# Mixer input projection by Strassen's scheme over 1024 tokens, attention beside the output projection of the chunk ahead

## Chip, cores and metric

The kernel runs on one core of a Trainium2 chip. The metric is the device time of one execution in microseconds; the time before is the median of three executions. One further execution was recorded by the profiler, and all rows of the profile come from it.

## The reference

One decoder layer for 2048 tokens of width 1024, all in float32. `w_in` has 4352 columns: queries (512), keys (128), values (128), three convolution inputs (512 each) and two gates (1024 each).

```python
def reference(x, mix_norm, w_in, b_in, sinks, conv_w, w_attn_branch, w_conv_branch, w_out,
              ffn_norm, w_up, ffn_conv_w, w_down, final_norm):
    h = x
    ...
        xn = rms_norm(h, mix_norm[l])
        proj = jnp.einsum("bsd,dp->bsp", xn, w_in[l]) + b_in[l]
        q, k, v, cb, cc, cx, ga, gc = jnp.split(proj, splits, axis=-1)
        attn = sliding_window_attention(q, k, v, sinks[l])
        conv = cb * causal_depthwise_conv(cc * cx, conv_w[l])
        merged = (jax.nn.sigmoid(ga) * jnp.einsum("bsc,cd->bsd", attn, w_attn_branch[l])
                  + jax.nn.sigmoid(gc) * jnp.einsum("bsc,cd->bsd", conv, w_conv_branch[l]))
        h = h + jnp.einsum("bsd,de->bse", merged, w_out[l])
        hn = rms_norm(h, ffn_norm[l])
        up = causal_depthwise_conv(jnp.einsum("bsd,df->bsf", hn, w_up[l]), ffn_conv_w[l])
        gate, val = jnp.split(up, 2, axis=-1)
        h = h + jnp.einsum("bsf,fd->bsd", jax.nn.silu(gate) * val, w_down[l])
    return rms_norm(h, final_norm)
```

Attention has 8 query heads on 2 key heads of width 64. Each block of 128 queries sees itself and the block before, under a band mask of 128 keys, and each head has a sink logit in its softmax. The convolutions are causal with three taps.

## The kernel before

Everything lies transposed: 128 channels on the partitions, tokens along the row. The sequence is worked in four chunks of 512 tokens; `k` counts the 8 slices of 128 channels of the width 1024. A float32 value is split into a high part, rounded to the type the matmul takes, and the rest (`split`, lines 221 to 223: a cast on ScalarE, a subtraction on VectorE). A product is then three matmuls, high by high, high by low and low by high (`mm3`, lines 197 to 199). Weights come as tiles of 128 columns (512 KB raw, 1 MB split); `order` lists them in the order of their use, `fetch` (line 121) loads and splits one, and `prefetch` runs two tiles ahead in the mixer and three in the feed-forward part. All transfers are issued on SyncE's queue (SP), one after the other. A scheduler places the instructions of each engine by its own model, so their order is near that of the code but not the same.

For each chunk `mixer` (line 466) projects keys, values and queries (`mixer_inputs`, line 320), then runs four blocks of attention: `scores` (line 373: scores and softmax), `weights_to_keys` (line 405: transposes of the weights and their split), `attend` (line 418: the product with the values). Between them stand the projections of the convolution inputs (`conv_tiles`, line 432). Eight branch steps follow, each with two gate projections (`gate`, line 460), the product of the convolution and that of the attention with the branch weights. `fillers` (line 506) slips in, beside the branch steps, the sums of squares of the next chunk and, in chunks 2 and 3, the operands of the up-projection of the first 1024 tokens (two slices in each). `out_proj` (line 530) adds x, stores h and normalizes it, and prepares the next chunk's input.

The up-projection already runs by the Strassen-Winograd scheme (`up`, line 608): over 1024 tokens a pair of weight tiles takes 7 products of 12 matmuls where plain products take 8. `up_operands` (line 564) forms the seven operands of the tokens by sums, splits them and stores them in DRAM; `load_up` (line 602) loads them as tiles of 2 MB, the first four ahead of the last output projection. The sums of weights are formed beside the products (`fetch_sums`). `down` (line 700) is plain; during its first half the operands of the second 1024 tokens are formed.

## Time and profile before

| | |
|---|---|
| median of three executions | 2550.72 us (2547.49 to 2550.80) |
| profiled execution, its own time | 2549.53 us |
| its span (first to last instruction) | 2547.8 us |
| mean granted clock of TensorE | 0.996 |
| transfers | 394.23 MB, 155 GB/s over the span |

The span leaves out some 2 us at the ends of an execution. Busy shares are means over stages with different limits, so a stage is read from its own stretch. In the page, PE is the matmul side of TensorE and PEld its weight loads, DVE is VectorE, ACT ScalarE, POOL GpSimd, and a row of a group ends with the idle time of the engine before it and what ended that.

### The profile page before, as it was taken

How to read it: one execution, taken by the hardware profiler on the slowest of the kernel's cores; microseconds unless marked ns; L12 is line 12 of the kernel's file. 1: busy time of each engine (PE TensorE's matmuls, PEld its weight loads, DVE VectorE, ACT ScalarE, POOL GpSimd, SP SyncE). 2: the span in 40 equal slices, each digit the busy share in tenths (PEclk: the TensorE clock that was granted, in tenths of full speed). 3: DMA queues.
4: the chain of work that ended last, by engine and by line, in shares of the span. 5: the costliest groups of instructions: out<-in, count | busy, mean ns of one | idle time of the engine just before them, and what ended most of it. 6: DMA issues, size and time to landing. Idle time of an engine off the chain costs nothing.

```text
span 2547.8 us, 29898 instructions
## 1 busy us (share of the span) xinstructions
PE 2525.5 (99%) x11404; PEld 2094.8 (82%) x11404; DVE 1711.5 (67%) x2093; ACT 1086.7 (43%) x1723; POOL 22.1 (1%) x73
## 2 busy tenths in 40 slices
PE   9999999999999999999999999999999999999998
PEld 7888888888888888887888888888888888888886
DVE  7954677446865568634798888755478888875335
ACT  6543455334653345432555555422135555551001
POOL 0000000000000000000000000000000000000000
PEclk9999999999999999999999999999999999999998
DMA  5243533335256442747443233888463333356421
GB/s 151 75 153 96 163 116 118 124 104 177 76 190 206 142 142 72 269 137 278 151 150 115 100 116 116 296 311 297 179 230 124 111 121 100 110 194 255 176 83 66
DMA packets 133631, 394.23 MB, mean 155 GB/s; under 512 B 15600, under 2 KB 16752, under 8 KB 128624
## 3 DMA queue, kind: packets, MB, share of 16 engines
q1 hardware_dynamic: 133488, 392.33, 45.5%
q8 instruction: 89, 1.46, 0.2%
q14 instruction: 54, 0.44, 0.1%
HBM read 291.61 MB, written 100.66 MB: 154 GB/s over the span
## 4 chain that ended last, share of the span: by engine, by line
PE 98%; issue 1%; DVE 0%; DMA 0%; ACT 0%; SPq 0%; POOLq 0%; POOL 0%; DVEq 0%; ACTq 0%
PE upx L620 6%; PE upx L622 6%; PE upx L621 6%; PE dn L197 6%; PE dn L199 6%; PE dn L198 6%; PE g L197 5%; PE g L199 5%; PE g L198 5%; PE upz L621 3%; PE upz L622 3%; PE upz L620 3%; PE wo L199 2%; PE wo L197 2%; PE wo L198 2%; PE upy L622 2%
## 5 line engine op out<-in xcount | busy, mean ns | idle before, releaser
L223 DVE TENSOR_TENSOR wh<-wr,wh 128x1024 fp32r<-128x1024 f32 (+1 forms) x250 | 298.6, 1197 | 228.3 <-ACT wh L222 226.3
L222 ACT CAST wh<-wr 128x1024 fp32r<-128x1024 f32 (+1 forms) x250 | 256.1, 1026 | 424.3 <-PE dn L199 214.4
L622 PE MATMUL upx<-upx,wh 128*128 128x512 f32 x704 | 275.8, 392 | 1.9 <-DVE wh L223 1.9
L620 PE MATMUL upx<-upx,wh 128*128 128x512 f32 x704 | 276.3, 393 | 0.0
L621 PE MATMUL upx<-upx,wh 128*128 128x512 f32 x704 | 275.6, 392 | 0.0
L197 PE MATMUL dn<-act,wh 128*128 128x512 f32 x704 | 274.2, 390 | 0.0
L199 PE MATMUL dn<-act,wh 128*128 128x512 f32 x704 | 274.0, 389 | 0.0
L198 PE MATMUL dn<-act,wh 128*128 128x512 f32 x704 | 273.9, 389 | 0.0
L713 DVE TENSOR_TENSOR hr<-dn,hr 128x512 f32<-128x512 f32 x192 | 131.3, 689 | 188.2 <-PE dn L199 188.0
L197 PE MATMUL g<-xnT,wh 128*128 128x512 f32 x512 | 200.1, 391 | 0.0
L199 PE MATMUL g<-xnT,wh 128*128 128x512 f32 x512 | 199.4, 389 | 0.0
L198 PE MATMUL g<-xnT,wh 128*128 128x512 f32 x512 | 199.3, 389 | 0.0
L622 PEld LDWEIGHTS upx<-upx,wh 128*128 128x128 f32 x704 | 132.5, 188 | 31.2 <-DVE wh L223 2.3
L620 PEld LDWEIGHTS upx<-upx,wh 128*128 128x128 f32 x704 | 132.5, 188 | 29.7 <-ACT uv L684 0.8
L621 PEld LDWEIGHTS upx<-upx,wh 128*128 128x128 f32 x704 | 132.6, 188 | 28.6
L199 PEld LDWEIGHTS dn<-act,wh 128*128 128x128 f32 x704 | 132.1, 188 | 27.7
L198 PEld LDWEIGHTS dn<-act,wh 128*128 128x128 f32 x704 | 132.2, 188 | 27.5
L197 PEld LDWEIGHTS dn<-act,wh 128*128 128x128 f32 x704 | 132.1, 188 | 27.1
L642 DVE SCALAR_TENSOR_TENSOR ag<-ug,fcwc,ag 128x1024 f32<-128x1024 f32 x88 | 113.0, 1284 | 52.4 <-ACT ag L640 50.8
L620 PE MATMUL upz<-upx,wh 128*128 128x512 f32 x352 | 137.0, 389 | 0.0
L622 PE MATMUL upz<-upx,wh 128*128 128x512 f32 x352 | 137.0, 389 | 0.0
L621 PE MATMUL upz<-upx,wh 128*128 128x512 f32 x352 | 137.0, 389 | 0.0
(231 smaller groups left out, 5132.2 us busy)
## 6 DMA issues: line engine op xcount, KB each, us to landing
wr<-in_w_dram SPq DMA_DIRECT2D x242, 512.0 KB, 3.7
act<-actd SPq DMA_DIRECT2D x20, 2048.0 KB, 9.5
upx<-upd SPq DMA_DIRECT2D x14, 2048.0 KB, 10.2
wra<-in_w_dram SPq DMA_DIRECT2D x44, 512.0 KB, 3.6
wrb<-in_w_dram SPq DMA_DIRECT2D x44, 512.0 KB, 3.6
actd<-ach SPq DMA_DIRECT2D x88, 256.0 KB, 2.2
actd<-acl SPq DMA_DIRECT2D x88, 256.0 KB, 2.4
upd<-uoh SPq DMA_DIRECT2D x56, 256.0 KB, 3.9
```

What stands on the lines that cost most here:

```text
L197: nc.tensor.matmul(ps, ah, bh, start=start, stop=False)
L198: nc.tensor.matmul(ps, ah, bl, start=False, stop=False)
L199: nc.tensor.matmul(ps, al, bh, start=False, stop=stop)
L222: nc.scalar.copy(out=dh, in_=src)
L223: nc.vector.tensor_sub(out=dl, in0=src, in1=dh.bitcast(F32))
L620: nc.tensor.matmul(bank, ah, bh, start=start and k == 0, stop=False, skip_group_check=True)
L621: nc.tensor.matmul(bank, ah, bl, start=False, stop=False, skip_group_check=True)
L622: nc.tensor.matmul(bank, al, bh, start=False, stop=stop and k == 3, skip_group_check=True)
L642: nc.vector.scalar_tensor_tensor(out=a, in0=u[:, k:k + 2 * T], scalar=w3[k], in1=a, op0=ALU.mult, op1=ALU.add)
L713: nc.vector.tensor_tensor(out=hs[n][j], in0=ps, in1=hs[n][j], op=ALU.add)
```

## The change

The input projection becomes a stage of its own ahead of the mixers. For the first 1024 tokens, keys, values, queries and two convolution tiles stay plain (`plain`); the other 26 tiles go as 13 Strassen pairs, and all 34 tiles of the second 1024 tokens as 17 pairs (`project_pairs`, through `strassen`, which `up` now uses as well). For this the normalized x is stored (`scale_x`) and the seven operands are formed from it in eight rounds of half chunks (`operands`). The sums of squares of the first two chunks go through small matmuls (`rms`). Queries, keys, values, the convolution's output and the sigmoids of the gates are stored in DRAM and loaded again by the mixers.

In the mixer of chunk c stand the attention of c, the output projection of chunk c − 1 and the products of the convolution with the branch weights; after the last block follow eight products of the attention (`attn_steps`). Half of the softmax scaling goes from VectorE to ScalarE. The split weights of the output projection are kept in DRAM and loaded from there from chunk 2's projection on. The operands of the up-projection of the first 1024 tokens are all formed beside the last output projection, and the first four operand tiles are loaded there slice by slice. The values' sign in the up-projection is taken at the copy out of PSUM, not in the taps' weights.

The orders, and the kept weights:

```diff
+MIX, LAST, FFN = 2, 6, 7
+PAIRS = ([(I_K, I_V), (I_Q, I_Q + 1), (I_Q + 2, I_Q + 3)]
+         + [(i + ct, i + ct + 1) for ct in (0, 2) for i in (I_CC, I_CX, I_CB)]
+         + [(I_GA + j, I_GC + j) for j in range(8)])
+PLAIN = [I_K, I_V] + [I_Q + j for j in range(4)] + [I_CC, I_CC + 1]
+FIRST = [list(range(4, len(PAIRS))), list(range(len(PAIRS)))]
...
+def _mixer_order(c):
+    out = [W_OUT + j for j in range(8)] if c else []
+    return out + [("conv", j) for j in range(8)] + [("attn", j) for j in range(8)]
...
+        cached = W_OUT <= i < W_OUT + 8
+        if cached and where > MIX + 1:
+            nc.sync.dma_start(out=t.bitcast(F32), in_=wo_d[i - W_OUT])
+            yield
+            return
...
+            if cached:
+                nc.sync.dma_start(out=wo_d[i - W_OUT], in_=t.bitcast(F32))
```

The plain part and the operands of the first 1024 tokens:

```diff
+    def scale_x(c, k, t, rb):
+        nc.vector.scalar_tensor_tensor(out=t, in0=t, scalar=g1c[:, k:k + 1], in1=rb, op0=ALU.mult, op1=ALU.mult)
+        nc.sync.dma_start(out=xn_d[c][k], in_=t)
...
+    def x_operands(d):
+        for k in range(4):
+            for h in range(2):
+                yield from operands(d, k, "x", xn_d, xop_d[d], slice(h * T // 2, (h + 1) * T // 2), "e", "e")
...
+        def rms(c):
+            ps = psum(f"ssa{c}")
+            for k in range(KD):
+                sq = tmp(f"sqa{c}_{k}")
+                nc.scalar.activation(out=sq, in_=st[c][:, k, :], func=AF.Square)
+                for t in range(NT):
+                    at = t * KD + k
+                    nc.tensor.matmul(ps[:, at:at + 1], sq[:, t * P:(t + 1) * P], ones, start=True, stop=True)
+            ss = p_s.tile([P, NT], F32, name=f"sum{c}", tag="sum")
+            nc.vector.tensor_reduce(out=ss, in_=ps[:, :NT * KD].rearrange("p (t k) -> p t k", t=NT), axis=AX.X, op=ALU.add)
+            return rstd(ss, f"a{c}")
...
+        def prepare():
+            for k in range(4):
+                for kk in (k, k + 4):
+                    for c in range(2):
+                        scale_x(c, kk, st[c][:, kk, :], rb[c])
+                    yield
+            yield from x_operands(0)
...
+        wkv = [wtile(0, I_K, 1), wtile(0, I_V, 1)]
+        kv0 = some(0, wkv, "kv")
+        wq = wtile(0, I_Q, 1)
+        p0 = some(0, [wq], "q")[0]
+        r = rms(0)
+        kv1 = some(1, wkv, "kv")
+        rb[0] = rstd_row(r, "a0")
+        take(0, kv0, p0)
+        p1 = some(1, [wq], "q")[0]
+        r = rms(1)
+        fill = prepare()
...
+        for j in range(1, 4):
+            wt = wtile(0, I_Q + j, 2 if j < 3 else 1)
+            for c in range(2):
+                p = some(c, [wt], f"q{j}_")[0]
+                if j == 1 and c == 0:
+                    rb[1] = rstd_row(r, "a1")
+                    take(1, kv1, p1)
+                take_q(c, j, scaled(p, rb[c], f"q{c}_{j}"))
+                steps(4)
```

The Strassen stage's start, the mixer and the last output projection:

```diff
+        xs = [load_x(xop_d[d], f"x{d}", i) for i in range(5)]
+        strassen(d, FIRST[d], xs, lambda: [load_x(xop_d[d], f"x{d}", i) for i in (5, 6)], begin, done, end, fill)
...
-            nc.vector.tensor_tensor(out=s[:, :, k0:256], in0=s[:, :, k0:256],
-                                    in1=rden[:, :, None].to_broadcast([P, G, 256 - k0]), op=ALU.mult)
+            if kv == 0:
+                nc.vector.tensor_tensor(out=s[:, :, k0:256], in0=s[:, :, k0:256],
+                                        in1=rden[:, :, None].to_broadcast([P, G, 256 - k0]), op=ALU.mult)
+            else:
+                for g in range(G):
+                    nc.scalar.activation(out=s[:, g, k0:256], in_=s[:, g, k0:256], func=AF.Copy, scale=rden[:, g:g + 1])
...
+    def attn_steps(c, attn, parts, merged):
+        nxt = gate(c, 0, 0)
+        for j in range(8):
+            sa, nxt = nxt, gate(c, j + 1, 0) if j < 7 else None
+            wt = wtile(MIX + c, ("attn", j))
...
+    def mixer(c, q, vT, conv, merged):
+        parts = p_16.tile([P, KD, T], F32, name=f"parts{c}", tag="t16")
         attn = p_16.tile([P, 2, 4, T], F32R, name=f"attn{c}", tag="t16")
-        conv = p_16.tile([P, 2, 4, T], F32R, name=f"conv{c}", tag="t16")
-        fill = conv_tiles(c, xT, rb, conv)
-        next(fill)
+        fill = conv_steps(c, conv, parts)
+        if c:
+            fill = chain(out_proj(c - 1, merged), fill)
+        def steps(n):
+            for _ in range(n):
+                next(fill, None)
+        plan = [0, 2, 1, 2, 1, 2, 2, 2, 2, 2] if c else [2, 1, 1, 0, 1, 0, 1, 0, 1, 1]
...
         attend(c, NT - 1, pts, attn)
-        filler = fillers(c)
+        for _ in fill:
+            pass
+        nxt = None
+        if c + 1 < NCH:
+            nxt = load_t16(q_d[c + 1], f"q{c + 1}"), load_kv(c + 1), load_t16(conv_d[c + 1], f"conv{c + 1}")
...
-        ups = up_operands(0, (c - 2) * 2, (c - 1) * 2) if c >= 2 else iter(())
...
+    def operands(d, k, name, src, dst, cs, big, split_to):
+        n_cs = cs.stop - cs.start
...
+        b1, b2 = get("b1_", big), get("b2_", big)
+        for t, i, n, kk in ((b1, 0, 0, k), (b1, 1, 1, k + 4), (b2, 0, 1, k), (b2, 1, 0, k + 4)):
+            nc.sync.dma_start(out=t[:, i, :], in_=src[2 * d + n][kk][:, cs])
...
-            if c + 1 == NCH:
-                xs = [load_up(0, i) for i in range(4)]
...
+        xs = [x_tile("upx0", i) for i in range(4)]
+        fill = up_operands(0, "b4", "b4")
+        done = 0
+        for _ in out_proj(NCH - 1, merged):
+            for _ in range(3):
+                if next(fill, fill) is not fill:
+                    done += 1
+                    if done % 5 == 0:
+                        k = done // 5 - 1
+                        for i, t in enumerate(xs):
+                            nc.sync.dma_start(out=t[:, :, k, :].bitcast(F32), in_=up_d[0][i][:, :, k, :])
```

The first place is SP's queue in the projection of the first tokens. Before, the queue there carries little but raw weight tiles (`wr`), for chunk 0's mixer:

```order
L133 DMA wr3_290<-in_w_dram 128x1024
L133 DMA wr4_368<-in_w_dram 128x1024
L133 DMA wr5_407<-in_w_dram 128x1024
L133 DMA wr6_467<-in_w_dram 128x1024
L133 DMA wr7_510<-in_w_dram 128x1024
L133 DMA wr8_548<-in_w_dram 128x1024
```

Now the last of the eight rounds of operands stands there: `xoh` and `xol` are split halves, `xopd0_i` is operand i in DRAM, `xb1` and `xb2` are the round's inputs from the stored normalized x (`xnd`), and `x0_i` are the loaded tiles. The rows show the end of round 7, the loads of round 8 and the end of round 8 with the first two tiles:

```order
L711 DMA xopd0_6_116<-xoh2_0_3_0_1389 128x256
L712 DMA xopd0_6_116<-xol2_0_3_0_1390 128x256
L716 DMA xb1_0_3_256_1397<-xnd0_3_81 128x256
L716 DMA xb1_0_3_256_1397<-xnd1_7_93 128x256
L716 DMA xb2_0_3_256_1398<-xnd1_3_89 128x256
L716 DMA xb2_0_3_256_1398<-xnd0_7_85 128x256
...
L711 DMA xopd0_2_112<-xoh2_0_3_256_1429 128x256
L712 DMA xopd0_2_112<-xol2_0_3_256_1430 128x256
L711 DMA xopd0_6_116<-xoh2_0_3_256_1429 128x256
L712 DMA xopd0_6_116<-xol2_0_3_256_1430 128x256
L743 DMA x0_0_1447<-xopd0_0_110 128x4096
L743 DMA x0_1_1449<-xopd0_1_111 128x4096
```

The loads of a round stand behind the stores of the round before, and the tiles behind the stores of the last round.

The second place is SP's queue at the last output projection. Before, the four operand tiles `upx0_0` to `upx0_3` are loaded whole, between weights (`wr`), ahead of the stores of h (`hd3`):

```order
L133 DMA wr194_9081<-in_w_dram 128x1024
L133 DMA wr195_9114<-in_w_dram 128x1024
L605 DMA upx0_0_9071<-upd0_0_142 128x4096
L605 DMA upx0_1_9073<-upd0_1_143 128x4096
L605 DMA upx0_2_9075<-upd0_2_144 128x4096
L605 DMA upx0_3_9077<-upd0_3_145 128x4096
L540 DMA hd3_0_102<-h3_0_9059 128x512
L540 DMA hd3_1_103<-h3_0_9059 128x512
```

Now slices of these tiles are loaded behind the stores of one slice's operands (`upd0`), the inputs of the next slice (`ub1`, `ub2`) follow, then x (`h3_3`) and a kept weight tile (`wod`):

```order
L711 DMA upd0_6_254<-uoh2_0_0_0_10089 128x512
L712 DMA upd0_6_254<-uol2_0_0_0_10090 128x512
L966 DMA upx0_0_9984<-upd0_0_248 128x2x512
L966 DMA upx0_1_9985<-upd0_1_249 128x2x512
L966 DMA upx0_2_9986<-upd0_2_250 128x2x512
L966 DMA upx0_3_9987<-upd0_3_251 128x2x512
L716 DMA ub1_0_1_0_10101<-hnd0_1_217 128x512
L716 DMA ub1_0_1_0_10101<-hnd1_5_229 128x512
L716 DMA ub2_0_1_0_10102<-hnd1_1_225 128x512
L716 DMA ub2_0_1_0_10102<-hnd0_5_221 128x512
L669 DMA h3_3_10107<-in_x_dram 128x512
L160 DMA wh221_10109<-wod5_181 128x2048
```

So stores of operands, loads of tiles, weights and h share this stretch of the queue.

The third place is TensorE behind the last attention block of chunk 1 (`po` is the product with the values). Before, a gate's projection stands ahead of it and the product of the convolution with the branch weights (`brc`) behind it:

```order
L199 MATMUL g1_26_3641<-xnT1_1_2287,wh69_3539 128x512
L425 MATMUL po1_3_0_3669<-pts1_3_0_0_3609,vt_193 128x512 x2
L425 MATMUL po1_3_0_3669<-pts1_3_0_1_3617,vt_193 128x512 x2
L425 MATMUL po1_3_1_3676<-pts1_3_1_0_3625,vt_193 128x512 x2
L425 MATMUL po1_3_1_3676<-pts1_3_1_1_3633,vt_193 128x512 x2
L197 MATMUL brc1_0_3696<-conv1_2820,wh70_3572 128x512
L198 MATMUL brc1_0_3696<-conv1_2820,wh70_3572 128x512
L199 MATMUL brc1_0_3696<-conv1_2820,wh70_3572 128x512
```

Now the convolution's last product stands ahead of it, and the product of the attention (`bra`, from `attn`) follows at once:

```order
L243 MATMUL brc1_7_7550<-conv1_6473,wh159_7440 128x512
L589 MATMUL po1_3_0_7565<-pts1_3_0_0_7489,vt_5892 128x512 x2
L589 MATMUL po1_3_0_7565<-pts1_3_0_1_7497,vt_5892 128x512 x2
L589 MATMUL po1_3_1_7572<-pts1_3_1_0_7505,vt_5892 128x512 x2
L589 MATMUL po1_3_1_7572<-pts1_3_1_1_7513,vt_5892 128x512 x2
L241 MATMUL bra1_0_7607<-attn1_6673,wh160_7465 128x512
L241 MATMUL bra1_1_7635<-attn1_6673,wh161_7522 128x512
L241 MATMUL bra1_2_7663<-attn1_6673,wh162_7545 128x512
L242 MATMUL bra1_0_7607<-attn1_6673,wh160_7465 128x512
L243 MATMUL bra1_0_7607<-attn1_6673,wh160_7465 128x512
```

What `bra` reads is the split of what `po` gives.

More of the change, by code (lines that the diff above doesn't have):

```diff
@@ L11 @@
 from contextlib import ExitStack
+from itertools import chain
 import concourse.bass as bass
@@ L110, in layer_kernel @@
              for d in range(2)]
-    order = [(c, i) for c in range(NCH) for i in _mixer_order()] + [(NCH + d, i) for d in range(2) for i in _ffn_order()]
+    order = _order()
     ready = {}
@@ L187, in prefetch @@
         while state["next"] <= min(last, len(order) - 1):
-            if order[state["next"]][0] >= NCH and order[state["next"]][1] != ("A", 0) and "e" not in pool:
+            i = order[state["next"]][1]
+            if "wrf" not in pool and isinstance(i, tuple) and i[0] in ("S21", "S3", "S4"):
                 break
@@ L287, in norm1_sums @@
         rstd_later(acc, f"a{c}", lambda rb: rows.update(rb=rb))
[L288 to L291 removed]
+        while not rows:
+            yield
         for k in range(KD):
@@ L472, in mixer @@
         ss = scores(c, q, 0)
-        for _ in range(3):
-            next(fill)
+        steps(plan[1])
         for b in range(1, NT):
@@ L530, in out_proj @@
[L530 to L542 removed]
+        for _ in fill:
+            pass
@@ L559, in norm2_back @@
             nc.sync.dma_start(out=hn_d[c][k], in_=t)
-        rstd_later(acc, f"b{c}", norm2, 1 if c + 1 < NCH else 3)
-        return xT
-    def up_operands(d, first, last):
-        big = "b4" if "b4" in pool else "u"
-        def get(name, tag, dt=F32):
-            return pool[tag].tile([P, 2, T], dt, name=f"{name}{d}_{k}", tag=tag)
+        nxt = load(0)
+        for j in range(KD):
+            h, nxt = nxt, load(j + 1) if j < KD - 1 else None
+            wt = wtile(MIX + c + 1, W_OUT + j)
+            ps = psum(f"wo{c}_{j}")
+            product(ps, wt, range(KD), pairs(merged[0]) + pairs(merged[1]))
+            nc.vector.tensor_tensor(out=h, in0=ps, in1=h, op=ALU.add)
+            nc.sync.dma_start(out=h_d[c][j], in_=h)
+            square_sum(acc, h, j)
+            if j == KD - 1:
+                rstd_later(acc, f"b{c}", norm2, 1 if c + 1 < NCH else 3)
+            yield
@@ L603, in load_up, with up_operands, x_tile @@
+        yield
+    def up_operands(d, big, split_to):
+        for k in range(4):
+            yield from operands(d, k, "u", hn_d, up_d[d], slice(0, T), big, split_to)
+    def x_tile(name, i):
         p = p_16 if i < 6 else pool["x7"]
-        t = p.tile([P, 2, 4, T], F32R, name=f"upx{d}_{i}", tag="t16" if i < 6 else "x7")
-        nc.sync.dma_start(out=t.bitcast(F32), in_=up_d[d][i])
-        return t
-    def up(d, xs):
-        c = NCH + d
-        xs.append(load_up(d, 4))
+        return p.tile([P, 2, 4, T], F32R, name=f"{name}_{i}", tag="t16" if i < 6 else "x7")
```

578 lines of the change are left out of this document (302 added, 276 removed).

## The prediction

> **What bounds the kernel now.** I read the head of the page first, then the shares of the chain that ended last, then the list of what TensorE waited for.
>
> ```profile
> span 2547.8 us, 29898 instructions
> PE 2525.5 (99%) x11404; PEld 2094.8 (82%) x11404; DVE 1711.5 (67%) x2093; ACT 1086.7 (43%) x1723; POOL 22.1 (1%) x73
> PE 98%; issue 1%; DVE 0%; DMA 0%; ACT 0%; SPq 0%; POOLq 0%; POOL 0%; DVEq 0%; ACTq 0%
> PE k L197 <- ACT xnT L230: 6.0, 1, 6.0
> PE wo L197 <- ACT wh L222: 2.4, 1, 2.4
> PE upx L622 <- DVE wh L223: 1.9, 1, 1.9
> PE wo L199 <- DVE wh L223: 0.5, 1, 0.5
> ```
>
> TensorE is busy 99% of the span, the chain is TensorE for 98%, and the list of its waits (us in total, times, longest) is short: only two places inside the kernel, the last output projection (2.4, 0.5) and the first Strassen products of the up-projection (1.9). So a matmul taken away counts in full, and so does every wait put in. What one matmul costs is the distance of two starts, not the 0.39 us of its row:
>
> ```profile
> 200.24 0.39 PE L197 MATMUL g<-xnT,wh 128*128 128x512 f32 x1
> ...
> 205.46 0.39 PE L199 MATMUL g<-xnT,wh 128*128 128x512 f32 x1
> ```
>
> Between these rows of the timeline lie 23 starts: 5.22 / 23 = 0.227 us each.
>
> **The change part by part.** The sum is made against the profiled execution, 2549.53 us (the span and 1.7 us around it); the median, 2550.72, is 1.2 above it, and the difference is left alone.
>
> *Matmuls taken away.* A projection tile of 128 columns and 512 tokens takes 8 slices of the inner dimension by 3 terms, 24 matmuls; 34 tiles by 4 chunks are 3264. Now 8 tiles over two chunks stay plain (384), and 13 pairs in the first Strassen stage and 17 in the second take 7 products of 12, 84 each (1092 and 1428): 2904. That is 360 fewer, by 0.227: **−81.6 us**. The first stage's sums of squares come by 64 matmuls of one column where 8 did before. From the chain's row
>
> ```profile
> 25.72 0.79 PE ssa L255 x8
> ```
>
> (four such matmuls with their weight loads) one takes 0.2 us, so 56 more are **+11**. If they were hidden by the transfers that the same stage waits for, they would cost nothing; I keep them, since they stand ahead of those transfers.
>
> *The wait ahead of the first Strassen pair.* The operands of the first stage cannot be formed before the second chunk's root mean square is known. By the matmuls that stand before it this is at about 61 us, and all plain matmuls are done at about 110. Between lie, in SP's order, 33 DMAs of other things, then 8 rounds of 4 loads and 14 stores of 128 KB (the loads of a round stand behind all stores of the round before), then the tile x0_0 of 2 MB. What SP takes for a DMA, and what a tile takes to land, show at the operands of before:
>
> ```profile
> 1694.08 0.45 SPq L579 DMA_DIRECT2D upd<-uoh  x1
> 1694.65 0.36 SPq L580 DMA_DIRECT2D upd<-uol  x1
> 1695.07 0.47 SPq L579 DMA_DIRECT2D upd<-uoh  x1
> ...
> upx<-upd SPq DMA_DIRECT2D x14, 2048.0 KB, 10.2
> upd<-uoh SPq DMA_DIRECT2D x56, 256.0 KB, 3.9
> ```
>
> About 0.45 us a DMA: 33 × 0.45 = 15, and 18 × 0.45 = 8.1 a round. Before the first store of a round can go, its loads land and are split; I take 3 us for that (a 256 KB store took 3.9 to land, and these are half as large), so 11 us a round. 61 + 15 + 8 × 11 + 8 for the tile = 172, less 110: 62 us of waiting. The next four tiles of the first pair land one behind the other, 2.1 MB each, about 5 us apart where a product takes 12 × 0.227 = 2.7: +8. Together **+70**. From below: the operands are 8 × 18 × 0.131 = 18.9 MB, the scaled inputs 4.2, weights and q, k, v 4.2, the tile 2.1, in all 29.4 MB. The fastest and a mixed stretch of the trace (columns: PE, PEld, DVE, ACT, POOL, clock, DMA share, GB/s)
>
> ```profile
> 1155.00:1160.00 5.00, 5.00 (x24) 4.14 (x23) 2.30 (x3) 0.91 (x2) 0.00 (x0) 1.00 1.01 428
> 1640.00:1660.00 20.00, 20.00 (x90) 16.57 (x89) 14.97 (x22) 2.62 (x3) 0.00 (x0) 1.00 1.01 376
> ```
>
> move 428 and 376 GB/s with all engines busy. At 428 the 29.4 MB take 69 us from 61 on: 20 us of waiting is the low end. The high end is 13 us a round, with the 3.9 us of a 256 KB store taken for the loads and some more for the split: 86.
>
> *The wait ahead of the first up-projection.* The operands of its first 1024 tokens were made in the mixers of chunks 2 and 3; now all are made inside the last output projection: 4 × 18 × 0.262 = 18.9 MB to and fro, 8.4 MB for the first four tiles, 4.2 for x and h, and 4.2 for four of the cached split weights (1 MB each, where 0.5 MB of raw weights was fetched). That is 35.7 MB; at 376 GB/s 95 us. TensorE has 192 matmuls, 43.5 us, and some 4 us of the branch product ahead of them, in which the first of these transfers already run, 48 in all: **+47**. At 428 it is +35. The stores that wait for splits on ScalarE and VectorE, between loads on one queue, make +70 the other end. By the Trainium skill, DMA: Bandwidth & Descriptors, section Where 436 GB/s comes from, transfers between HBM and SBUF are bound at about 358 GB/s by the core's share of the HBM; an estimate from it is 100 − 48 = 52 us here. The trace does not agree, since its row shows 428, so the sum goes by the rows.
>
> *The mixers.* The same attention now stands beside less work of TensorE. By groups, VectorE needs for it
>
> ```profile
> L223 DVE TENSOR_TENSOR pts<-pt,pts 128x512 fp32r<-128x512 f32 x62 | 39.9, 676 | 12.5 <-ACT pts L222 12.5
> L387 DVE SCALAR_TENSOR_TENSOR s<-sc,mask 128x512 f32<-128x512 f32 x60 | 37.2, 684 | 33.3 <-PE sc L386 33.3
> L401 DVE TENSOR_TENSOR s<-s,rden 128x1024 f32<-128x1024 f32 x30 | 36.5, 1217 | 0.2
> L396 DVE TENSOR_REDUCE m<-s 128x4 f32<-128x1028 f32 x30 | 35.2, 1213 | 0.0
> L428 DVE TENSOR_TENSOR o<-po,o 64x512 f32<-64x512 f32 x32 | 21.9, 685 | 0.5
> L223 DVE TENSOR_TENSOR attn<-o,attn 128x512 fp32r<-128x512 f32 x16 | 11.0, 684 | 0.7 <-ACT attn L222 0.7
> L222 ACT CAST attn<-o 128x512 fp32r<-128x512 f32 x16 | 9.9, 620 | 16.7 <-DVE o L428 16.7
> L427 ACT COPY o<-po 64x512 f32<-64x512 f32 x32 | 18.6, 582 | 0.8
> L223 DVE TENSOR_TENSOR wh<-ws,wh 128x512 fp32r<-128x512 f32 x44 | 30.5, 692 | 0.0
> ```
>
> A quarter of the sums, the 36.5 halved since half of that scaling moves to ScalarE, is 41 us a chunk. In chunk 0, beside it stand 8 convolution steps, each a split of half a tile (0.69) and a product with the gate (0.69): 11, and 2 for the values and reciprocals, 54 in all. TensorE has 96 matmuls there (21.8) and attention; the chain's rows
>
> ```profile
> 89.45 1.75 PE pt L412 x16
> ...
> 96.70 1.87 PE po L425 x8
> ```
>
> and 1.9 for the scores give 5.5 a block, 20 in all: 42. So VectorE bounds chunk 0: +12 by the sums, **+20** with hand-offs, between 12 and 30. In chunks 1 to 3 the output projection of the chunk ahead joins: TensorE has 43.6 + 21.8 + 22 + 2 = 89 us. VectorE has 54 and 17 for residual, squares and norm (8 of 0.69 each), 71, and 10 more where the projection's weights aren't cached yet, by the group
>
> ```profile
> L223 DVE TENSOR_TENSOR wh<-wr,wh 128x1024 fp32r<-128x1024 f32 x242 | 295.6, 1222 | 224.1 <-ACT wh L222 222.1 <-DMA upd<-uol 0.6
> ```
>
> (8 × 1.22). So the sums leave TensorE the bound, and what counts is the end: the product with the attention follows the last block at once, where the convolution's product and a gate's projection (12 and 24 matmuls) stood between. Copy, add, cast and subtraction are 0.58 + 0.69 + 0.62 + 0.68 = 2.6, with semaphores some 3.3 us, and what the clock does after such a stop shows in
>
> ```profile
> 1175.00:1180.00 5.00, 2.10 (x7) 1.29 (x7) 3.75 (x4) 2.51 (x3) 0.00 (x0) 0.96 0.25 67
> 1180.00:1190.00 10.00, 10.00 (x39) 8.11 (x38) 3.65 (x4) 3.09 (x4) 0.00 (x0) 0.85 0.61 194
> ```
>
> 2.9 us without a matmul, then a granted clock of 0.85 over 10 us, a loss near 1.6. With a block that lags, 7 us for each of three mixers: **+21**, between 6 (the chain alone hidden in part) and 40. By the Trainium skill, TensorE: Matmul & The Clock Gate, section HAM oscillation, only idle gaps above about 3.4 us halve the clock. Here 2.9 us did already; by the rule the three tails would be some 5 us cheaper and the sum 2632.
>
> *The rest.* Twice a new stage starts with five tiles of 2 MB behind its predecessor's last reads: **+8**, between 0 and 20. The old waits at the last output projection and the first up-projection, with the clock after them, go: 2.4 + 0.5 + 1.9 + 2 × 1.6 = **−8**. The sum of squares on VectorE, the stores of q, k, v, convolution and gates (hidden under 570 us of Strassen products, which stand to these stores as they did to those of before) and the sign by a scale instead of by the weights cost nothing; without cover each store's 0.45 us on SP would show.
>
> Sum: −82 + 11 + 70 + 47 + 20 + 21 + 8 − 8 = **+87**, 2549.5 + 87 = **2637 us**.
>
> **The rivals.** *TensorE waits for bytes alone.* SP runs ahead of the splits, both transfer stages stream at 428 GB/s, and the attention stays hidden, as in before, where the list has no wait of TensorE inside a mixer. Then −82 + 11 + 20 + 35 + 0 − 8 = −24: 2526 us, faster. It decides where all new waits together stay under 82 − 11 + 8 = 79 us. For it speaks the row of 428; against it that loads of a round stand behind stores that wait for splits, and that even its two stages leave only 24 of 79 us for four mixers.
> *The attention bounds all mixers.* If VectorE's 71 to 81 us in chunks 1 to 3 come in lumps, each of the 12 blocks there loses some 3 us and the clock is halved about half of the time: +20 for each mixer and +20 more for chunk 0, 2637 + 60 = 2697. Against it: ScalarE takes half of the scaling, and 89 us of matmuls cover the sums.
> *The projection does not do less.* That the pairs saved nothing (2637 + 82 = 2719) the order of TensorE excludes: 84 matmuls stand in a pair.
> *One stage is covered.* If the operands take 7 us a round and not 11, the first wait falls from 70 to 38: 2605; with 428 GB/s at the last output projection as well, 2593.
>
> **How the numbers follow.** Forecast, 2600 to 2680: 0.60. One or both stages covered, 2556 to 2600: 0.13. Attention bounds the mixers or both waits at their upper ends, above 2680: 0.13. Within 0.2% of before (about what a measurement of this kernel can tell from no change): 0.04. Bytes alone, faster: 0.10. The range for 8 in 10 leaves out most of the last and the far end of the heavy case: 2570 to 2705. Faster 0.10, same 0.04, slower 0.86.
>
> **What would show it.** The list of waits: a wait for DMA of some 60 us ahead of the first product on x0_0, and a second of 40 or more ahead of the first on upx0_0; TensorE's busy time down by about 70; SP issuing 8 rounds of operands with gaps at each load. The windows: VectorE above 90% in chunk 0's mixer, the clock below 1.00 behind each last attention block. I am wrong if the first operand round takes 7 us or less, if these stages wait for nothing, or if a wait stands where I have none: inside the Strassen stages, whose three raw weight tiles and 0.45 us stores share one queue.

## The result, and the profile after

The changed kernel takes 2726.4 us (median of four, 2724.6 to 2728.2) beside 2549.2 before: 1.0695 times as long, 95% interval 1.0677 to 1.0714. It was forecast slower, 2637 with a range to 2705; it lies 21 us above the range, and the loss of 177 us is twice the 87 of the sum.

The head of the page and the shares of the chain of the changed kernel:

```profile
span 2723.7 us, 30965 instructions
PE 2505.4 (92%) x11156; PEld 2063.2 (76%) x11156; DVE 1786.0 (66%) x2309; ACT 1126.3 (41%) x1859; POOL 21.8 (1%) x72
PE 77%; DMA 8%; DVE 5%; ACT 4%; SPq 3%; issue 3%; DVEq 0%; POOLq 0%; POOL 0%; ACTq 0%
```

TensorE's share falls from 99% to 92%: it now stands idle for 218 us of the span, where it was 22. These 196 us are more than the 176 by which the span grew, since its busy time fell by 20; but 360 matmuls less are 82.

The list of what TensorE waited for (us in total, times, longest), its upper rows:

```profile
PE upx L756 <- DMA x<-xopd: 95.9, 3, 88.5
PE wo L241 <- DMA wh<-wod: 23.3, 3, 10.2
PE upx L756 <- ACT wh L258: 21.8, 2, 16.1
PE bra L241 <- ACT attn L258: 14.0, 4, 5.0
PE upx L756 <- DMA upx<-upd: 11.8, 2, 11.6
PE vp L530 <- DMA vT<-vd: 7.3, 1, 7.3
```

The operand tiles of the projection (`x`) lead, with one wait of 88.5 us; then come the last output projection and the first up-projection (9.8 + 3.4 + 10.2 by the kept weights, 16.1 by the split of a weight tile, 11.6 by an operand tile, all within 80 us of the span), and the four tails of the mixers (`bra`). These places were in the forecast. Three smaller ones were not: 5.7 us (in the third row, with the 16.1) inside the first Strassen stage, where the prediction named a wait as a sign of being wrong, 7.3 for the values ahead of the first mixer (`vp`), and 3.4 ahead of the second chunk's sums of squares.

Nor was the loss that the windows show (PE, PEld, DVE, ACT, POOL, granted clock, DMA share, GB/s):

```profile
23.70:32.40 8.70, 8.70 (x57) 8.67 (x56) 2.39 (x3) 0.97 (x2) 0.00 (x0) 0.70 0.63 192
32.40:37.30 4.90, 4.90 (x13) 3.84 (x14) 0.00 (x0) 0.00 (x0) 0.00 (x0) 0.50 0.00 0
61.00:78.00 17.00, 16.88 (x72) 16.21 (x73) 3.33 (x6) 4.24 (x8) 0.00 (x0) 0.51 0.61 196
...
0.00:133.20 133.20, 120.98 (x520) 101.92 (x520) 55.50 (x86) 43.46 (x69) 2.87 (x12) 0.88 0.58 179
133.20:221.60 88.40, 0.00 (x0) 0.00 (x1) 33.16 (x56) 18.67 (x33) 0.00 (x0) 0.52 0.68 214
...
1276.00:1365.00 89.00, 49.54 (x193) 39.20 (x191) 23.96 (x32) 13.19 (x18) 0.00 (x0) 0.79 0.98 343
```

In the plain part the clock falls to half while TensorE is fully busy: in both runs of one-column matmuls that form the sums of squares, and behind them. (TensorE had stood still for 1.7 us ahead of the first run and 3.4 us ahead of the second, so these rows alone don't tell the run from the stop.) TensorE's busy time times one minus the granted clock, summed in steps of 4 us over the whole span, is 42 us; in the kernel before it is 4. That is the busy time lost to the clock. The third group reads differently: in the 88 us of the first wait the DMA engines are two thirds busy, at the last output projection they are full.

Why the first pair came so late shows on the queues. The rows are TensorE's transposes that spread the second chunk's root mean square, SP's first loads of a round, the loads of the fourth, one later round (loads, first store, next loads), the loads of the tiles, and the first product:

```profile
83.55 0.60 PE L304 MATMUL rba<-ident,ra 128*128 128x128 f32 x4
...
106.14 1.96 SPq L716 DMA_DIRECT2D xb<-xnd  x4
...
154.23 1.89 SPq L716 DMA_DIRECT2D xb<-xnd  x4
...
165.78 1.89 SPq L716 DMA_DIRECT2D xb<-xnd  x4
170.70 0.32 SPq L711 DMA_DIRECT2D xopd<-xoh  x1
...
178.21 1.90 SPq L716 DMA_DIRECT2D xb<-xnd  x4
...
213.50 2.65 SPq L743 DMA_DIRECT2D x<-xopd  x5
...
221.63 0.76 PE L756 MATMUL upx<-x,wh 128*128 128x512 f32 x1 [88.49 <-DMA x<-xopd]
```

The root mean square is known at 84 us, not 61; the first round starts at 106, not 76; eight rounds to 213.5 are 13.4 us each, not 11. The first three, between whose stores SP also issues stores of queries, take 16.0 each (106.14 to 154.23); the other five take 11.9 (to 213.50), and the one shown 12.4: 4.9 from its loads to its first store, 7.5 for its stores. Only the tile's 8 us were as forecast.

### The profile page after: what moved, and what is told of

Read it like the earlier page. It is cut to its first block, busy times and chain, and to the rows that moved or that the text cites. A ratio compares the mean times of both kernels' runs of the same rounds, so it can differ in the third digit from the quotient of the medians.

```text
span 2723.7 us, 30965 instructions
## 1 busy us (share of the span) xinstructions
PE 2505.4 (92%) x11156; PEld 2063.2 (76%) x11156; DVE 1786.0 (66%) x2309; ACT 1126.3 (41%) x1859; POOL 21.8 (1%) x72
## 4 chain that ended last, share of the span: by engine, by line
PE 77%; DMA 8%; DVE 5%; ACT 4%; SPq 3%; issue 3%; DVEq 0%; POOLq 0%; POOL 0%; ACTq 0%
PE upx L756 9%; PE upx L758 9%; PE upx L757 9%; PE dn L243 6%; PE dn L241 6%; PE dn L242 6%; PE upz L756 5%; PE upz L758 4%; PE upz L757 4%; PE upy L756 2%; PE upy L757 2%; PE upy L758 2%; PE wo L243 1%; PE wo L241 1%; PE wo L242 1%
## 5 line engine op out<-in xcount | busy, mean ns | idle before, releaser
L756 PE MATMUL upx<-upx,wh 128*128 128x512 f32 x704 | 276.4, 393 | 29.4 <-ACT wh L258 16.1
L756 PE MATMUL upx<-x,wh 128*128 128x512 f32 x480 | 191.6, 399 | 103.8 <-DMA x<-xopd 95.9
L817 DVE SCALAR_TENSOR_TENSOR a<-u,fcwc,a 128x1024 f32<-128x1024 f32 x176 | 224.4, 1283 | 51.4 <-ACT a L815 48.7
L758 PE MATMUL upx<-x,wh 128*128 128x512 f32 x480 | 189.3, 395 | 0.4 <-DVE wh L259 0.4
L757 PE MATMUL upx<-x,wh 128*128 128x512 f32 x480 | 189.5, 395 | 0.0
L756 PEld LDWEIGHTS upx<-x,wh 128*128 128x128 f32 x480 | 91.8, 191 | 127.1 <-issue 94.8
L258 ACT CAST wh<-ws 128x1024 fp32r<-128x1024 f32 (+1 forms) x148 | 123.3, 836 | 152.3 <-DVE ws L201 66.2
L259 DVE TENSOR_TENSOR wh<-ws,wh 128x1024 fp32r<-128x1024 f32 (+1 forms) x148 | 141.0, 956 | 62.0 <-ACT wh L258 61.9
L258 ACT CAST wh<-wr 128x1024 fp32r<-128x1024 f32 (+1 forms) x66 | 63.5, 972 | 284.8 <-PE dn L243 218.6
L756 PE MATMUL upz<-upx,wh 128*128 128x512 f32 x352 | 137.3, 390 | 0.0
```

The source lines that it names most:

```text
L258: nc.scalar.copy(out=dh, in_=src)
L259: nc.vector.tensor_sub(out=dl, in0=src, in1=dh.bitcast(F32))
L756: nc.tensor.matmul(bank, ah, bh, start=start and k == 0, stop=False, skip_group_check=True)
L757: nc.tensor.matmul(bank, ah, bl, start=False, stop=False, skip_group_check=True)
L758: nc.tensor.matmul(bank, al, bh, start=False, stop=stop and k == 3, skip_group_check=True)
L817: nc.vector.scalar_tensor_tensor(out=a, in0=u[:, k:k + 2 * T], scalar=w3[k], in1=a, op0=ALU.mult, op1=ALU.add)
```

## The experiments

Theory and rival are those of the expectation that stands ahead of each result. All are edits of the changed kernel but one; each time stands beside the kernel before on the same chip, 2547 to 2548 us there. The wait of the first pair varies little from run to run (88.5, 87.8, 87.9 and 87.9 us in the four profiles that share the plain part).

**Sums of squares as before** (`e1_sums`): squares on ScalarE, sums on VectorE, four one-column matmuls a chunk in place of 32.

```diff
-                    nc.tensor.matmul(ps[:, at:at + 1], sq[:, t * P:(t + 1) * P], ones, start=True, stop=True)
...
+            acc = row_tile(f"acca{c}", "acc")
+            for k in range(KD):
+                square_sum(acc, st[c][:, k, :], k)
+            return rstd_tokens(acc, f"a{c}")
```

> Sums of squares of the first two chunks on ScalarE and VectorE again, with 4 one-column matmuls a chunk in place of 32. Theory (the runs of one-column matmuls halve the granted clock, and the second one puts off the root mean square on which all operands wait): no half clock between 24 and 84 us, the plain matmuls end some 20 us earlier (113 in place of 133) and the first operand loads start some 20 us earlier (86 in place of 106), so the first pair starts near 200 and the time falls by about 20 us, to 2706. Rival (SP's queue, with the stores of queries between the rounds, sets the start of the first pair whatever the plain part does): the plain part ends earlier, the wait grows by the same, and the time stays at 2726.

2716.2 us, 10 less: half of what was expected. The first pair starts at 210 and not 222, and its wait is 89.3, so start and end of the wait move together and the rival falls. The busy time lost to the clock in the plain part falls from 15 us to 5. But the sums now came late from VectorE (first row; the second is the first pair):

```profile
62.41 1.84 PE L288 MATMUL ssa<-ones,acca 128*128 128x1 f32 x8 [11.43 <-DVE acca L276]
...
210.12 0.76 PE L750 MATMUL upx<-x,wh 128*128 128x512 f32 x1 [89.29 <-DMA x<-xopd]
```

**One-column matmuls alone** (`h1_ones`), in the kernel before, in a stretch where TensorE never waits:

```diff
+            pz = psum("one")
+            for k in range(8):
+                for t in range(4):
+                    nc.tensor.matmul(pz[:, t * 8 + k:t * 8 + k + 1], q[:, 0, k % 4, t * P:(t + 1) * P].bitcast(F32), ones, start=True, stop=True)
```

> The kernel before, with 32 one-column matmuls on the queries put into the busy stretch of chunk 1's mixer (their result goes nowhere). Theory (a run of one-column matmuls by itself lets the clock gate halve the clock): the granted clock in that stretch falls to 0.5 for 4 us or more though TensorE never waits, and the time grows by 9 to 16 us. Rival (the clock falls for the idle gap that stood ahead of such runs in the changed kernel): the clock stays at 1.00 and the time grows by 32 x 0.2 = 6 to 7 us.

2561.2 us, 1.0052 times before (1.0039 to 1.0066), so 10 to 17 us more. The timeline and the windows of this run:

```profile
340.08 2.73 PE L472 MATMUL one<-ones,q 128*128 128x1 f32 x24
...
344.39 4.82 PE L472 MATMUL one<-ones,q 128*128 128x1 f32 x40
349.08 0.77 PE L198 MATMUL cc<-xnT,wh 128*128 128x512 f32 x1
```

```profile
346.00:349.00 3.00, 3.00 (x27) 3.00 (x26) 0.00 (x0) 0.00 (x0) 0.00 (x0) 0.91 0.02 8
349.00:352.00 3.00, 3.00 (x9) 2.42 (x9) 0.19 (x1) 0.00 (x0) 0.00 (x0) 0.52 0.02 5
352.00:355.00 3.00, 3.00 (x17) 2.52 (x17) 0.00 (x0) 0.43 (x1) 0.00 (x0) 1.00 0.00 0
```

The longer piece (each matmul has two records) is followed by 3 us at half clock, the shorter by none; no idle time stands ahead of either or between them. So the run itself lowers the clock, and the theory holds, though 3 us are less than its 4. The profiled execution (2554.7) is 7 us above the kernel before, which is also the rival's size, so it is the clock that decides there; the others are 11 to 16 above, with a mean granted clock of 0.994 to 0.995 in place of 0.997.

**Four gate pairs plain** (`e2_plain4`), ahead of the first Strassen pair, with the filling steps of the Strassen stage denser to match:

```diff
+NG = 4
+PLAIN = [I_K, I_V] + [I_Q + j for j in range(4)] + [I_CC, I_CC + 1] + [i + j for j in range(NG) for i in (I_GA, I_GC)]
+FIRST = [[*range(4, 9), *range(9 + NG, len(PAIRS))], list(range(len(PAIRS)))]
```

> Four of the gate pairs of the first 1024 tokens are projected plainly, ahead of the first Strassen pair: 8 tiles x 2 chunks x 24 = 384 plain matmuls (87 us) in place of 4 x 84 = 336. Theory (the first wait is a fixed chain of transfers that TensorE could fill): the wait of 88.5 falls to 0 to 10, the 48 matmuls more cost 11, so about -70 to -75 us: 2650 to 2655. Rival (the same transfers only move on: the first Strassen stage is 76 us shorter and no longer hides the inputs and operands of the second 1024 tokens): the wait comes back ahead of the second stage, 30 to 60 us, and the time is 2680 to 2715.

2708.8 us: the rival. The first wait falls from 88.5 us to 10.9, and the second stage's operands become the next one:

```profile
244.09 0.76 PE L766 MATMUL upx<-x,wh 128*128 128x512 f32 x1 [10.89 <-DMA x<-xopd]
...
487.13 0.80 PE L766 MATMUL upx<-x,wh 128*128 128x512 f32 x1 [30.35 <-DMA x<-xopd]
```

**Loads of a round on GpSimd's queue** (`e5_queue`), **and half of its stores too** (`e7_queue2`):

```diff
+            (nc.gpsimd if name == "x" else nc.sync).dma_start(out=t[:, i, :], in_=src[2 * d + n][kk][:, cs])
...
+                (nc.gpsimd if name == "x" else nc.sync).dma_start(out=dst[place][:, 1, k, cs], in_=lo[:, i, :].bitcast(F32))
```

> The four loads of each operand round of the Strassen input stages are issued on GpSimd's queue; all else stays on SP's. Theory (a round of 12 us is 7.5 us of 14 stores on SP's queue and 4.5 us in which that queue stands still for the next loads and the first sums): the loads run ahead, a round takes 8 us, the first wait falls by 8 x 4 = 32, to 55, and the second stage's operands come earlier as well: 2680 to 2695. Rival (a round is bound by VectorE's and ScalarE's steps or by buffers): the round stays at 11 to 12 us, the time at 2720 to 2730.

> As the run before, and the stores of the low halves go on GpSimd's queue too, 7 of the 14 of a round. If SP's 0.5 us for a store is what is left, a round falls to 4.5 to 5.5 us and the first wait to 30 to 40: 2650 to 2670. If the bytes are (2.4 MB a round in rows of 1 KB; at share 0.65 the engines moved 196 GB/s, so some 300 at most), a round stays at 8 us or more, and this run is within 8 us of the one before.

2720.9 and 2736.1 us. With the loads alone on GpSimd's queue the first wait falls from 88.5 us to 75.8, where the theory had 55, and a round takes 10.4 us instead of 11.9 (147.84 to 189.37 for four), not 8. With both edits the wait is 80.2; SP has 7 stores a round left, and still two rounds of GpSimd's queue lie 22.5 us apart. The first three rows are of the first run, the last two of the second:

```profile
147.84 2.16 POOL L716 DMA_DIRECT2D xb<-xnd  x4 [12.15 <-DVE xol L259]
157.91 2.16 POOL L716 DMA_DIRECT2D xb<-xnd  x4 [7.91 <-DMA xopd<-xol]
...
189.37 2.16 POOL L716 DMA_DIRECT2D xb<-xnd  x4 [9.02 <-ACT cc L448]
```

```profile
172.87 2.17 POOL L716 DMA_DIRECT2D xb<-xnd  x4
...
195.41 2.17 POOL L716 DMA_DIRECT2D xb<-xnd  x4
```

That is 11.3 us a round. So SP's queue accounts for 1.5 us of a round and not for most of it, and the theory falls. Nor do the bytes: in a window of the second run the DMA engines are busy for 0.64.

```profile
150.00:205.00 55.00, 0.00 (x0) 0.00 (x0) 20.93 (x38) 13.34 (x24) 28.83 (x55) 0.50 0.64 206
```

VectorE (20.9 of 55 us) and ScalarE aren't full either. By exclusion the chain is left, from landing through sums, splits and stores to free buffers. The idle times in the first run's rows point the same way: GpSimd's queue, which has nothing else to issue there, stands still for some 8 us or more ahead of each round's loads, behind splits (`xol`), behind stores that have yet to land (`xopd`) or behind a step of the plain part (`cc`), and all tiles of a round come from one pool of 7 buffers (`e`). No run enlarged that pool, so this stays argued; the run after next leaves the loads out. Nor was it separated why the second run is 15 us above the first; up to 22 us of waits of Strassen products for VectorE and ScalarE stand there, 16 in the first run and 2 in the changed kernel.

**First stage plain** (`e8_no0`): all 34 tiles of the first 1024 tokens plain, the inputs and operands of the second formed beside them.

```diff
-        fill = prepare()
+        fill = chain(norm1(2), norm1(3), x_operands(1))
...
-        o += [(d, i) for i in _pair_order(FIRST[d])]
+    o += [(0, i) for i in TILES]
+    o += [(1, i) for i in _pair_order(FIRST[1])]
```

> All 34 tiles of the first 1024 tokens are projected plainly, so no operands are formed from them and the first Strassen stage is gone; the second stays. 156 more matmuls are +35 us. Theory (the first stage costs more by its wait than it saves by its products): the waits ahead of and inside the first pairs (96 us and 6 of clock) go, and the plain stage of 370 us hides the inputs and operands of the second 1024 tokens: 2640 to 2665. Rival (the transfers of the front part bind as a whole): 30 to 60 us come back inside or behind the plain stage, 2690 or more.

2652.0 us, as the theory had it: 74 less with 156 matmuls more. So the first stage as built costs some 110 us (74 + 35) beside the 35 us that its products save.

**Operands from SBUF** (`e9_adirect`): the scaled x is used where it lies; no stores of x, no loads of rounds.

```diff
-                        scale_x(c, kk, st[c][:, kk, :], rb[c])
...
-            yield from x_operands(0)
+                a, b, p, q = st[0][:, k, :], st[1][:, k, :], st[0][:, k + 4, :], st[1][:, k + 4, :]
...
+                nc.vector.tensor_tensor(out=t0, in0=a, in1=b, op=ALU.subtract)
+                nc.vector.tensor_tensor(out=t1, in0=q, in1=b, op=ALU.subtract)
+                put(p, 1, k)
```

> The operands of the first Strassen stage are formed from the scaled x where it lies in SBUF: no stores of x, no loads of rounds, 4 rounds of 14 stores of 256 KB. Theory (the first wait is the chain of eight rounds, each load, sums, splits, stores and the next load when its buffers come free): the 56 stores take 28 us of SP's queue and VectorE's sums and splits some 45, so x0_0 lands at 140 to 150 where TensorE runs dry at 133: the wait falls from 88 to 10 to 20, the time to 2650 to 2665. Rival (bytes and the order of the whole front part bind, as in the run with four plain pairs): 30 us or more come back later, 2685 or more.

2666.7 us, 60 less, 2 us above what the theory gave. The same products run, and the wait is a third of what it was (the theory had 10 to 20 us):

```profile
163.77 0.77 PE L780 MATMUL upx<-x,wh 128*128 128x512 f32 x1 [28.59 <-DMA x<-xopd]
```

In that wait the engines are full (share 1.01, 358 GB/s):

```profile
135.00:164.00 29.00, 0.41 (x2) 0.26 (x2) 19.03 (x28) 11.11 (x18) 0.00 (x0) 0.56 1.01 358
```

So the round trip of x through DRAM made two thirds of the first wait; what is left is a stretch in which the bytes bind. The edit takes loads, stores and the halving of rows out together; which of them counts most isn't told apart.

**Operands of the up-projection beside the attention products again** (`e3_up_early`), two slices in each of chunks 2 and 3:

```diff
+            for _ in range(2 if c >= 2 else 0):
+                next(ups[c - 2], None)
...
+        xs = [load_x(up_d[0], "upx0", i) for i in range(4)]
```

> The operands of the first up-projection are formed beside the attention products of chunks 2 and 3 again, two slices in each, and its first four tiles are loaded whole. Theory (the last output projection waits for 35 MB): the waits there and ahead of the first up product (52 us, and 10 us of clock behind them) fall to 10 or less; the two attention stages of 22 us take 9.4 MB more each and grow by 10 to 15: 2690 to 2700. Rival (the waits are the order of the queue at the end, tiles behind stores, not bytes): the loads of kept weights and of tiles still wait, under 20 us gained: above 2706.

2722.6 us. The time is the rival's, its reason is not: the waits ahead of the first up product are gone, but the attention products of chunks 2 and 3 now wait for their weights, and the last output projection still waits for kept weights (4.4 and 10.1 us).

```profile
1170.92 0.80 PE L241 MATMUL bra<-attn,wh 128*128 128x512 f32 x1 [10.28 <-ACT wh L258]
...
1308.48 0.80 PE L241 MATMUL bra<-attn,wh 128*128 128x512 f32 x1 [6.07 <-ACT wh L258]
...
1354.50 0.79 PE L241 MATMUL wo<-mg,wh 128*128 128x512 f32 x1 [10.06 <-DMA wh<-wod]
```

**Four of the seven operands without DRAM** (`e10_bdirect`): in the last output projection operands 0 to 3 are split into the tiles that the products read.

```diff
+            for i, place in enumerate(places):
+                if place < len(direct):
+                    t = direct[place]
+                    split(t[:, 0, k, :], t[:, 1, k, :], src[:, i, :])
...
+        fill = up_operands(0, "b4", "b4", xs)
```

> In the last output projection, operands 0 to 3 of the first up-projection are split straight into the tiles that the products read; only 4 to 6 go through DRAM. That takes 8.4 MB of stores and 8.4 MB of loads out of some 36 MB. Theory (bytes bind there: share 0.98 from 1276 to 1365 us): 19 MB at 376 GB/s are 50 us beside 48 of TensorE, so the waits of 52 us and the clock behind them (10) fall to 5 to 15: 2675 to 2690. Rival (the order of the queue or VectorE binds): less than 20 us gained, 2706 or more.

2681.3 us, 45 less, as the theory had it: the waits of 52 us there are 13 now. Moving the transfers (the run before) gave 4 us, taking them away 45. The edit takes away their bytes and their places in SP's queue together; that the bytes count rests on the full DMA engines of the changed kernel there (share 0.98).

**The tails** (`e4_tail`): one or two products of the convolution behind the last block.

```diff
-        plan = [0, 2, 1, 2, 1, 2, 2, 2, 2, 2] if c else [2, 1, 1, 0, 1, 0, 1, 0, 1, 1]
+        plan = [0, 2, 1, 2, 1, 2, 2, 2, 1, 1] if c else [2, 1, 1, 0, 1, 0, 1, 0, 1, 0]
```

> In each mixer one or two of the convolution's products stand between the last block's product with the values and the first product of the attention, in place of ahead of it; nothing else moves. Theory (the chain copy, add, cast, subtract is bare): the four waits of the attention products for the split (14 us) and the half clock behind them (some 4 us) go: 2708 to 2712. Rival (the blocks before it have lost the cover, so the last block's own splits come late): no change beyond 5 us, 2721 to 2731.

2717.3 and 2732.3 us in two executions: no change that can be told. The waits for the attention's split fall to 1.2 us, and the next product waits for the split of its weights in their place:

```profile
902.45 1.20 PE L241 MATMUL bra<-attn,wh 128*128 128x512 f32 x4 [1.23 <-ACT attn L258]
...
1028.76 0.79 PE L241 MATMUL bra<-attn,wh 128*128 128x512 f32 x1 [5.14 <-ACT wh L258]
...
1150.65 0.64 PE L241 MATMUL bra<-attn,wh 128*128 128x512 f32 x1 [4.98 <-ACT wh L258]
```

Neither what was expected nor the rival's reason; what those weights wait for was not separated.

**Both ways around DRAM, and early sums** (`e11_all`), the edits of `e9_adirect` and `e10_bdirect` and the sums of squares on ScalarE and VectorE, begun right behind the loads; **and with two gate pairs plain** (`e12_all_plain2`).

> Both changes of the two runs before, and the sums of squares on ScalarE and VectorE begun right after the loads of x. Theory (three separate losses): -70, -45 and -12 add up, 2590 to 2610; what stays above the kernel before is the mixers, the changes of stage and the splits of the plain part. Rival (what one part gains another waits for): 2640 or more.

> The run with all three repairs, and two of the gate pairs of the first 1024 tokens projected plainly ahead of the first Strassen pair: 192 plain matmuls in place of 168. Theory (what is left of the first wait, 30 us, is time in which TensorE could work): 24 more matmuls cost 5.4 us, the wait and the half clock behind it go, 2565 to 2580. Rival (as with four plain pairs: the first Strassen stage, two pairs shorter, no longer hides the inputs and operands of the second 1024 tokens): 20 us or more come back ahead of the second stage, 2585 or more.

2595.4 us (1.0194, 1.0177 to 1.0211) and 2592.3 (1.0168, 1.0151 to 1.0185). The three losses add up: 131 less, where 60, 45 and 10 were measured one by one (the sums begin sooner than in their own run). The second run has the rival's time, and no difference from the first that can be told; its place is another. The first wait, 29.9 in the run before, is gone, and much of it comes back inside the plain part and the shorter Strassen stage, mostly in waits for weights (one of 9.9 us, one of 4.1 and three of 3), not ahead of the second stage: TensorE's idle time falls by only 10 us, from 110 to 100. Both stay above the kernel before; no version beat it. In the first of them TensorE's busy time is 45 us below the kernel before, its idle time 88 above.

## Why the prediction was wrong

*What bounds the kernel* was right: with TensorE at 99%, every wait put in counted. *The matmuls* were right: 2520 in the Strassen pairs and 384 plain, 360 less. *The side and the main places* were right: the two transfer stages and the mixers' tails are among the waits that the list shows, with VectorE above 90% in chunk 0's mixer (36.3 of the 38 us from 850 on), as forecast.

The miss of 89 us has two parts. In waits the sum had 156 (70, 47, 41 less the 5 of clock in it, 8, less the 5 of the old ones), and 196 were measured. In busy time it had −69 (−82, +11, 5 of clock, less 3 of the old), and −20 was measured; the sign "TensorE's busy time down by about 70" did not come. Two steps failed above all: the clock, which the sum prices only behind the mixers' tails, and the 15 us and 8 rounds of 11 us between the root mean square and the first tile.

- **The wait ahead of the first pair** was mis-sized: 70 in the sum, measured 96 (88.5, 1.9, and 5.7 in the second pair for a weight tile that took 16 us to land behind the operand tiles). The steps that failed are "33 × 0.45 = 15", measured 22 from the root mean square to the first loads, and "so 11 us a round", eight of which took 107 and not 88, 15 of the 19 us more in the three rounds that share SP's queue with stores of queries. These 26 us are what the wait of 88.5 has above the 62 of the sum. The reason for the rounds failed as well: "about 0.45 us a DMA" on SP's queue and 3 us in between came near the size of an undisturbed round (11 for 11.9), but with other queues a round still took 10.4 to 11.3. Two thirds of the wait were the round trip through DRAM, shown by leaving it out.
- **The start.** "By the matmuls that stand before it this is at about 61 us" failed too: the sums of squares ran largely at half clock, and the root mean square came at 84. But TensorE ran dry 23 us late as well, at 133 and not 110, so this put off the first pair and left the length of its wait as it was; with the sums as before, too, the pair started 12 us earlier and waited 89.3.
- **One-column matmuls** were priced at 0.2 us from a row of four at full clock, +11. A run of 32 lowers the clock, and 15 of the 23 us by which the plain part ended late are busy time lost to the clock. Taking the runs out gained 10 us.
- **The clock** stood in the sum for the mixers' tails alone, with 5 us. It was lost in the plain part and behind most of the long waits, 37 us more than before. With the matmuls (−82) and the 56 one-column ones at the 0.23 us each of the row of 12 in `h1_ones` (+13) that makes −32 and leaves 12 us of the busy time unplaced.
- **The wait ahead of the up-projection** was right in mechanism and near in size: 47, measured 52. The DMA engines are full there, moving the transfers gave 4 us and leaving them out 45. The measured rate is 343 GB/s over 89 us at share 0.98, where the sum took 376.
- **The mixers** were priced at 41; the waits there (14.0 for the split of the attention, 4.7 and 1.1 for weights, some 6 inside the blocks) and the clock behind them, some 5, are 30. Putting products of the convolution behind the last block (`e4_tail`) gained nothing that can be told: the weights were next.
- **The changes of stage**, 8, were 15: 8 ahead of the second Strassen stage and 7.3 for the values of the first mixer, a load that the sum left out.
- By the Trainium skill, TensorE: Matmul & The Clock Gate, section HAM oscillation, the clock halves at idle gaps above some 3.4 us. Of the four tails here, a gap of 2.66 us at 891 us was followed by a granted clock of 0.65 over 8 us, one of 2.77 at 1011 and one of 3.56 at 1131 by no lower clock, and one of 4.98 at 1252 by 0.57 over 4 us. Two of the four went as the rule has it (2.77 and 4.98); ahead of the first pair's third product a gap of 1.91 us was followed by 0.57 over 4 us, and one-column matmuls lowered the clock without a gap. The prediction's own price came from "2.9 us without a matmul" in the kernel before, which were two gaps, 2.38 and 0.53 us. Neither that price nor the rule gives the tails' clock.

```profile
892.00:900.00 8.00, 8.00 (x24) 6.32 (x25) 2.25 (x4) 0.62 (x1) 0.00 (x0) 0.65 0.34 110
1007.00:1019.00 12.00, 9.23 (x41) 7.19 (x40) 5.07 (x9) 2.65 (x5) 0.00 (x0) 1.00 1.00 373
1127.00:1139.00 12.00, 8.44 (x37) 6.54 (x37) 5.49 (x9) 2.69 (x5) 0.00 (x0) 1.00 0.98 366
1252.00:1256.00 4.00, 3.67 (x9) 2.90 (x10) 4.00 (x6) 2.18 (x3) 0.00 (x0) 0.57 0.78 273
231.40:235.40 4.00, 3.98 (x11) 3.14 (x12) 0.45 (x1) 0.00 (x0) 0.00 (x0) 0.57 0.99 426
```

What stays open: what sets a round within the chain through DRAM, why the attention's weights are late in the mixers, and the 12 us of busy time.

## What to carry to other kernels

Where one engine is at 99%, taking instructions from it pays only if forming the new operands costs it less in waits: here 82 us of matmuls stood against 196 us of waits, and the largest two were trips through DRAM whose source or target lay in SBUF. A transfer that is only moved to another stage comes back as the wait of that stage (four plain pairs, the early operands) or of one near it (the last run); it is gained where the bytes or the chain are taken away. And the time at which a chain can start deserves the same care as its rate, in the right place of the sum: here the late sums of squares put off the start by 23 us and lengthened the work ahead of the wait by as much, while the wait itself grew by the rounds and by what stood in front of them.

## What the runs showed of the hardware

A long enough run of one-column matmuls lowered the granted clock without any idle time: 20 of them in 4.8 us were followed by 3 us at half clock, 12 in 2.7 us were not, and 28 in 8.7 us, with a gap of 1.7 us ahead, had the clock at 0.70 during the run and 0.50 in the 4.9 us behind it. The length of a stop did not settle what the clock did behind it: after stops of 1.91, 2.66 and 4.98 us it was at 0.57 to 0.65 over the next 4 to 8 us, after 2.77 and 3.56 us at 1.00. Issuing a dependent round's loads, or loads and half of the stores, on GpSimd's queue in place of SP's changed its period little: 10.4 and 11.3 us for 11.9.
